# One weight tile in four of a feed-forward stage: its lower part by an accumulating DMA instead of a VectorE subtraction

## The chip, the cores and the metric

The kernel runs on one core of a Trainium2 chip. A core has five engines with queues of their own: TensorE (PE; PEld is its loading of the stationary operand), VectorE (DVE), ScalarE (ACT), GpSimd (POOL) and SyncE (SP, which here only starts DMAs). 16 DMA engines move data between the chip's memory and the core's SBUF. The metric is the time of one execution on the device in microseconds (us); less is better.

## The reference

One layer of a hybrid decoder over 256 positions with a model width of 2048, all in float32. A state-space group and an attention group work on one joint input projection and share an output projection; then comes a feed-forward part with a short causal convolution between its two matrices, then a gated embedding. The part that matters here:

```
a    = RMSNorm(h)
h    = h + concat(ssd_heads, attn_heads) @ W_out
g, u = split(causal_dwconv3(RMSNorm(h) @ W_up))       # W_up: 2048 x 11264
h    = h + (SiLU(g) * u) @ W_down                     # W_down: 5632 x 2048
h    = h + sigmoid(RMSNorm(h) @ W_pg) * RMSNorm(p @ W_pe)
```

## The kernel before

**Split products.** TensorE works on float32r, a rounded float32. To keep the precision of float32, each operand is split into a rounded upper part and the rest, the lower part, and three products are added: upper × upper, upper × lower and lower × upper. The activations are split once and stay in SBUF (`Lhs`, hi and lo). The weights are split tile by tile as they arrive.

**A weight tile.** `load_w` fetches 128 partitions x 1024 floats (512 KB): two blocks of 128 rows by 512 columns of a weight matrix. SP starts the load into `w`, for which there are `WR` = 7 buffers. `split` then has ScalarE copy it, rounding, to `wh` (line 192), and VectorE subtract: `wl = w - wh` (line 193). `wh` and `wl` have `WB` = 4 buffers each. `products` issues 12 matmuls of 512 columns for a tile: 2 blocks × 2 halves of the positions × 3 products (lines 222 to 224: upper × `wh`, upper × `wl`, lower × `wh`).

**A chunk.** `gemm` runs a list of tiles into one pair of PSUM accumulators (one for each 128 positions; two such pairs exist). In the up projection a chunk is 512 columns of W_up: eight tiles, numbered s = 0 to 7. There are 22 chunks, 11 for g and 11 for u. After a chunk, `up` scales the accumulators to `u` on ScalarE (line 879), and GpSimd separates the 16-bit halves into `half` (line 881). SP starts two DMA transposes into `flip` (line 883), GpSimd puts the halves together again in `uc` (line 884), and ScalarE and VectorE do the convolution (lines 286 and 288). For a pair of chunks GpSimd multiplies SiLU(g) by u (line 904), and the result is split for the down projection.

**Segments.** `SEGS` = 2, 2, 2, 2, 2, 1 pairs of chunks. The down projection of a segment (`project`: four columns of 512, with four tiles each for two pairs and two tiles each for one) is taken up after the chunks of the next segment; the last one follows at the end, in a call of its own.

**Order.** Each engine carries out its queue in order. In this stage the order in each queue is made by a scheduler when the program is built: it simulates the program in time and gives each engine what is ready. A buffer's next writer waits until its last reader is done. Only the attention stage and the start have TensorE's order written by hand.

Of the kernel before, what the change touches and what calls it, by code (L numbers as in the profile page):

```python
# [11 lines left out]
F32 = mybir.dt.float32  # L12
# [3 lines left out]
AF = mybir.ActivationFunctionType  # L16
ALU = mybir.AluOpType
# [7 lines left out]
KT = D // P  # L25
EPS = 1e-6
NC = 512
KG = 4
KW = 2
# [36 lines left out]
def hybrid_layer(  # L66
# [20 lines left out]
    nc = tc.nc  # L87
    V, S, G, PE = nc.vector, nc.scalar, nc.gpsimd, nc.tensor
# [19 lines left out]
    def sb(pool, shape, tag, dt=F32, bufs=None):  # L108
        kw = {} if bufs is None else {"bufs": bufs}
        size = math.prod(shape[1:]) * (2 if dt in (mybir.dt.bfloat16, U16) else 4)  # L110
        tags = sizes.setdefault(pool.id, {})
        tags[tag] = max(tags.get(tag, 0), -(-size // 32) * 32 * (bufs or pool.bufs))
        return pool.tile(shape, dt, tag=tag, name=nm(tag), **kw)
# [7 lines left out]
    def acc_pair():  # L121
        return [ps_acc.tile([P, NC], F32, tag=f"acc{b}", name=nm(f"acc{b}")) for b in range(NB)]
# [17 lines left out]
    def load_first(k, pieces=1):  # L140

        xt = sb(xin, [P, T], "xt", bufs=6)
        nc.sync.dma_start(xt, xT[:, k, :])
        w = sb(wp, [P, KW, NC], "w", bufs=WR)
        n = KW // pieces
        for c in range(0, KW, n):
            cs = slice(c, c + n)
            nc.sync.dma_start(w[:, cs, :], w_in[cs, k // KW, :, (k % KW) * NC : (k % KW + 1) * NC].rearrange("c p n -> p c n"))
        return w, xt
# [40 lines left out]
    def split(src, hi, lo, scale=None):  # L190
        if scale is None:
            S.copy(hi, src)  # L192
            V.tensor_tensor(out=lo, in0=src, in1=hi.bitcast(F32), op=ALU.subtract)  # L193
        else:
            S.activation(out=hi, in_=src, func=AF.Copy, scale=scale)
            V.scalar_tensor_tensor(out=lo, in0=src, scalar=scale, in1=hi.bitcast(F32), op0=ALU.mult, op1=ALU.subtract)

    def load_w(src, kt=KW, pieces=1):

        w = sb(wp, [P, KW, NC], "w", bufs=WR)  # L200
        wh = sb(wp, [P, KW, NC], "wh", F32R)
        wl = sb(wp, [P, KW, NC], "wl", F32R)
        n = kt * NC // pieces
        w2, wh2, wl2 = (t.rearrange("p a b -> p (a b)") for t in (w, wh, wl))
        for i in range(pieces):
            s = slice(i * n, (i + 1) * n)
            nc.sync.dma_start(w2[:, s], src[:, s])
            split(w2[:, s], wh2[:, s], wl2[:, s])
        return wh, wl

    def products(acc, lhs, w, k0, kt, total, apart=False, halves=False, whole=None):

        wh, wl = w
        order = [(i, b) for i in range(kt) for b in range(NB)]
        if apart:
            order.sort(key=lambda ib: ib[1])
        if halves:
            order = order[:kt]
        for i, b in order:
            k = k0 + i  # L220
            hi, lo = lhs(k, b)
            PE.matmul(acc[b], lhsT=hi, rhs=wh[:, i, :], start=(k == 0), stop=False)  # L222
            PE.matmul(acc[b], lhsT=hi, rhs=wl[:, i, :], start=False, stop=False)  # L223
            PE.matmul(acc[b], lhsT=lo, rhs=wh[:, i, :], start=False, stop=(k == total - 1 or (b == NB - 1 and k + 1 == whole)))  # L224
        if halves:
            b = NB - 1
            for c in range(0, NC, NC // 2):
                cs = slice(c, c + NC // 2)
                for i in range(kt):
                    hi, lo = lhs(k0 + i, b)  # L230
                    for left, right in ((hi, wh), (hi, wl), (lo, wh)):
                        PE.matmul(
                            acc[b][:, cs],
                            lhsT=left,
                            rhs=right[:, i, cs],
                            start=False,
                            stop=True,
                            skip_group_check=True,
                        )

    def gemm(acc, lhs, srcs, halves=False):

        for s, src in enumerate(srcs):
            last = s == len(srcs) - 1
            total = len(srcs) * KW
            products(acc, lhs, load_w(src), s * KW, KW, total, last, last and halves, total - KW if halves else None)

    class Lhs:

# [59 lines left out]
    def v3(a, m):  # L309
        return a.rearrange("p (a b) -> p a b", a=m)  # L310
# [7 lines left out]
    with xin_:  # L318
# [21 lines left out]
        for k in range(KT):  # L340
            w, xt = first[k] if k < len(first) else load_first(k)
# [6 lines left out]
            wh = sb(wp, [P, KW, NC], "wh", F32R)  # L348
            wl = sb(wp, [P, KW, NC], "wl", F32R)
            n = 1 if k < 3 else KW  # L350
# [12 lines left out]
            if k in (5, 9):  # L363
                b = k // 4 - 1
# [15 lines left out]
    def in_chunk(c):  # L380
        acc = acc_pair()
        gemm(acc, aT, [w_in[c, g] for g in range(KT // KW)])
        return acc

    def evac_scaled(acc, pool, tag, bufs=None):
        res = []
        for b in range(NB):
            t = sb(pool, [P, NC], f"{tag}{b}", bufs=bufs)
            S.activation(out=t, in_=acc[b], func=AF.Copy, scale=rx[:, b : b + 1])
            res.append(t)  # L390
        return res

    def add_to_h(acc, n):
        for b in range(NB):
            hs = hres[b][:, n * NC : (n + 1) * NC]
            V.tensor_tensor(out=hs, in0=hs, in1=acc[b], op=ALU.add)  # L396
# [10 lines left out]
        V.tensor_reduce(out=s1, in_=ss, axis=AX.X, op=ALU.add)  # L407
        return rstd(s1, D, NB, tag)

    def project(lhs, w, i0, ni, after=None):  # L410

        for n in range(4):
            acc = acc_pair()
            gemm(acc, lhs, [w[i, n] for i in range(i0 * KG // KW, (i0 + ni) * KG // KW)])
            add_to_h(acc, n)
            if after:
                after(n)
# [3 lines left out]
    with tc.tile_pool(name="ssd", bufs=1) as sp, tc.tile_pool(name="dram", bufs=1, space=bass.MemoryType.DRAM) as dp:  # L421
        BT = sb(sp, [P, 4, T], "BT")
        CT = sb(sp, [P, 4, T], "CT")
        for c, (acc, dst, tag) in enumerate(((acc_b, BT, "ct"), (acc_c, CT, "Xd"))):
            t = evac_scaled(acc, sp, tag, 1)
# [9 lines left out]
        for b in range(NB):  # L435
            V.scalar_tensor_tensor(
                out=u[:, :, b, :], in0=v3(tr[:, b * 32 : (b + 1) * 32], 4), scalar=rx[:, b : b + 1], in1=v3(dtb, 4), op0=ALU.mult, op1=ALU.add
# [21 lines left out]
        for b in range(NB):  # L459
            V.scalar_tensor_tensor(  # L460
                out=adt4[:, :, b, :], in0=dt4[:, :, b, :], scalar=-1.0, in1=v3(ea, 4), op0=ALU.mult, op1=ALU.mult
# [174 lines left out]
    hT = Lhs(act, KT, "a")  # L636
# [234 lines left out]
    with tc.tile_pool(name="ffn", bufs=2) as fp:  # L871

        def up(c):
            acc = acc_pair()
            gemm(acc, hT, [w_up[c, g] for g in range(KT // KW)])
            uc = sb(fp, [P, 4, T], "uc", bufs=1)
            for b in range(NB):
                u_ = sb(fp, [P, NC], f"u{b}", bufs=1)
                S.activation(out=u_, in_=acc[b], func=AF.Copy, scale=rh[:, b : b + 1])  # L879
                half = sb(fp, [P, 2 * NC], f"half{b}", U16, 1)  # L880
                G.tensor_copy(half.rearrange("p (a n) -> p a n", a=2), u_.bitcast(U16).rearrange("p (n a) -> p a n", a=2))  # L881
                flip = sb(fp, [P, 8, P], f"flip{b}", U16, 1)
                nc.sync.dma_start_transpose(flip, half)
                G.tensor_copy(  # L884
                    uc[:, :, b * P : (b + 1) * P].bitcast(U16).rearrange("p f (t a) -> p f t a", a=2),
                    flip.rearrange("p (a f) t -> p f t a", a=2),
                )
            cv = sb(fp, [P, 4, T], f"cv{c // NPAIR}", bufs=2 - c // NPAIR)
            for f in range(4):
                w = fcw[:, (4 * c + f) * 4 : (4 * c + f + 1) * 4]  # L890
                conv_tile(uc[:, f, :], cv[:, f, :], [w[:, j : j + 1] for j in range(3)], w[:, 3:4])
            return cv

        pair = 0
        pending = []
        ssg = sb(small, [P, NB, 4], "ssg", bufs=1)

        for s, np_ in enumerate(SEGS):
            gT = Lhs(fp, KG * np_, "g")
            for i in range(np_):  # L900
                cg = up(pair + i)
                S.activation(out=cg, in_=cg, func=AF.Silu)
                cu = up(NPAIR + pair + i)
                G.tensor_tensor(out=cg, in0=cg, in1=cu, op=ALU.mult)
                split(cg, gT.t[i][0], gT.t[i][1])
            if pending:
                project(*pending.pop())
            pending.append((gT, w_down, pair, np_))
            pair += np_
        h2T = Lhs(act, KT, "a")  # L910
        project(*pending.pop(), lambda n: next_lhs(h2T, ssg, n, g_ple))
        embed()
    rg = finish_rstd(ssg, "rg")


    with tc.tile_pool(name="ple", bufs=2) as lp:
# [5 lines left out]
        for n in range(4):  # L922
            acc = acc_pair()
# [77 lines left out]
```

## Time and profile before

| | |
|---|---|
| Median of 3 runs | 1433.31 us (1432.83 to 1434.88) |
| Profiled execution, its span | 1434.9 us |
| TensorE matmul busy | 1423.2 us (99%) |
| VectorE, ScalarE, GpSimd busy | 984.1, 804.2, 286.2 us |
| HBM read, written | 268.32 MB, 2.13 MB |

The span is the time from the first to the last instruction of the profiled execution, 1434.9 us, which is its own time here, against the runs' median of 1433.31 us. In the lists below, a group of instructions has a line number of the kernel, an engine, an operation, the tiles written and read, its count, its busy time with the mean length in ns of one, and the idle time of the engine just before them with what ended it. A timeline row has the start and length in us. A matmul's length there is that of the whole pipeline; TensorE issues the next one before it is over.

### The profile page before, as it was taken

What the parts mean: (1) busy time and instruction counts of PE and PEld (TensorE: products, weight loads), DVE (VectorE), ACT (ScalarE), POOL (GpSimd) and SP (SyncE); (2) the same over time, 40 slices, a digit from 0 to 9 for tenths busy, and PEclk for the clock granted to TensorE, in tenths of its full rate; (3) what the DMA queues carried; (4) which work ended last, traced back from release to release, by engine and by line L of the source; (5) the groups of instructions that cost most, each with busy time, mean ns of one, the idle gap of its engine ahead of it and who ended that gap; (6) DMA issues with size and microseconds to landing.
All of it is one profiled execution on the core that took longest, in us unless ns stands there. A gap on an engine that the chain in (4) does not pass through costs nothing.

```text
span 1434.9 us, 18092 instructions
## 1 busy us (share of the span) xinstructions
PE 1423.2 (99%) x6527; PEld 1167.3 (81%) x6527; DVE 984.1 (69%) x1242; ACT 804.2 (56%) x1101; POOL 286.2 (20%) x212
## 2 busy tenths in 40 slices
PE   9999999999999999999999999999999999999998
PEld 7887888888787778888888888888888888888887
DVE  6678876776678897656667646765675576476854
ACT  6675555644567666556556446545554554455643
POOL 0002010008345432013243112201320131120000
PEclk9999999999999999999999999999999999999999
DMA  9656656548687778577887767867876877776671
GB/s 332 236 173 198 215 177 185 171 148 223 188 220 187 209 220 220 168 211 207 219 226 202 217 205 206 225 196 198 230 208 192 223 201 218 206 208 190 208 226 65
DMA packets 163467, 292.62 MB, mean 204 GB/s; under 512 B 93041, under 2 KB 95921, under 8 KB 162993
## 3 DMA queue, kind: packets, MB, share of 16 engines
q1 hardware_dynamic: 162944, 290.99, 70.5%
q8 instruction: 51, 0.84, 0.2%
q10 hardware_dynamic: 432, 0.48, 0.1%
q14 instruction: 40, 0.32, 0.1%
HBM read 268.32 MB, written 2.13 MB: 188 GB/s over the span
## 4 chain that ended last, share of the span: by engine, by line
PE 68%; DVE 1%; ACT 0%; issue 0%; POOL 0%; DVEq 0%; ACTq 0%
PE acc L222 22%; PE acc L224 22%; PE acc L223 22%; PE tr L779 1%; PE tr L272 0%; PE sc L738 0%; DVE wl L193 0%; ACT s L753 0%; DVE nm L749 0%; DVE s L742 0%; ACT wh L192 0%; DVE sg L931 0%; ACT s L761 0%; DVE qkr L672 0%; DVE h L396 0%
## 5 line engine op out<-in xcount | busy, mean ns | idle before, releaser
L193 DVE TENSOR_TENSOR wl<-w,wh 128x1024 fp32r<-128x1024 f32 (+1 forms) x495 | 634.9, 1288 | 378.5 <-ACT wh L192 376.4
L192 ACT CAST wh<-w 128x1024 fp32r<-128x1024 f32 (+1 forms) x495 | 514.8, 1045 | 480.7 <-PE acc L224 431.4
L223 PE MATMUL acc<-wl,ah 128*128 128x512 f32 x1278 | 500.1, 391 | 1.5 <-DVE wl L193 1.5
L224 PE MATMUL acc<-wh,al 128*128 128x512 f32 x1278 | 499.0, 391 | 0.0
L222 PE MATMUL acc<-wh,ah 128*128 128x512 f32 x1278 | 498.3, 392 | 0.0
L223 PEld LDWEIGHTS acc<-wl,ah 128*128 128x128 f32 x1278 | 240.1, 188 | 52.3 <-DVE wl L193 2.4
L222 PEld LDWEIGHTS acc<-wh,ah 128*128 128x128 f32 x1278 | 240.1, 188 | 51.0 <-issue 1.4
L224 PEld LDWEIGHTS acc<-wh,al 128*128 128x128 f32 x1278 | 240.1, 188 | 50.1 <-issue 0.7
L224 PE MATMUL acc<-wh,gl 128*128 128x512 f32 x352 | 137.1, 390 | 0.0
L223 PE MATMUL acc<-wl,gh 128*128 128x512 f32 x352 | 137.1, 390 | 0.0
L222 PE MATMUL acc<-wh,gh 128*128 128x512 f32 x352 | 136.5, 390 | 0.0
L881 POOL COPY half<-u 128x1024 uint16<-128x1024 uint16 x44 | 62.0, 1422 | 264.3 <-ACT u L879 264.3
L222 PE MATMUL acc<-wh,yh 128*128 128x512 f32 x256 | 101.6, 397 | 0.6 <-DVE h L396 0.6
L223 PE MATMUL acc<-wl,yh 128*128 128x512 f32 x256 | 99.9, 390 | 0.0
L224 PE MATMUL acc<-wh,yl 128*128 128x512 f32 x256 | 99.7, 390 | 0.0
L884 POOL COPY uc<-flip 128x1024 uint16<-128x1024 uint16 x44 | 54.9, 1248 | 177.2 <-DMA flip<-half 174.9
L223 PEld LDWEIGHTS acc<-wl,gh 128*128 128x128 f32 x352 | 66.1, 188 | 13.7
L224 PEld LDWEIGHTS acc<-wh,gl 128*128 128x128 f32 x352 | 66.1, 188 | 13.6
L222 PEld LDWEIGHTS acc<-wh,gh 128*128 128x128 f32 x352 | 66.1, 188 | 13.6
L288 DVE SCALAR_TENSOR_TENSOR cv<-uc,fcw,cv 128x254 f32<-128x254 f32 (+1 forms) x176 | 73.2, 476 | 3.4 <-ACT cv L286 3.4
L396 DVE TENSOR_TENSOR h<-h,acc 128x512 f32<-128x512 f32 x112 | 73.0, 678 | 1.8 <-PE acc L224 1.8
L222 PEld LDWEIGHTS acc<-wh,yh 128*128 128x128 f32 x256 | 48.1, 188 | 14.6 <-issue 2.0
(239 smaller groups left out, 1129.2 us busy)
## 6 DMA issues: line engine op xcount, KB each, us to landing
w<-in_w_up_dram SPq DMA_DIRECT2D x176, 512.0 KB, 4.2
w<-in_w_in_dram SPq DMA_DIRECT2D x126, 512.0 KB, 4.2
w<-in_w_down_dram SPq DMA_DIRECT2D x88, 512.0 KB, 4.3
w<-in_w_out_dram SPq DMA_DIRECT2D x64, 512.0 KB, 4.2
w<-in_w_pg_dram SPq DMA_DIRECT2D x32, 512.0 KB, 4.3
seg<-scr SPq DMA_DIRECT2D x8, 512.0 KB, 5.0
xt<-in_xT_dram SPq DMA_DIRECT2D x16, 128.0 KB, 7.0
h<-in_x_dram SPq DMA_DIRECT2D x2, 1024.0 KB, 8.7
```

Of the source, the lines that this page charges most:

```text
L192: S.copy(hi, src)
L193: V.tensor_tensor(out=lo, in0=src, in1=hi.bitcast(F32), op=ALU.subtract)
L222: PE.matmul(acc[b], lhsT=hi, rhs=wh[:, i, :], start=(k == 0), stop=False)
L223: PE.matmul(acc[b], lhsT=hi, rhs=wl[:, i, :], start=False, stop=False)
L224: PE.matmul(acc[b], lhsT=lo, rhs=wh[:, i, :], start=False, stop=(k == total - 1 or (b == NB - 1 and k + 1 == whole)))
L288: V.scalar_tensor_tensor(out=dst[:, s:], in0=ps[:, : T - s], scalar=taps[n - 1 - s], in1=dst[:, s:], op0=ALU.mult, op1=ALU.add)
L396: V.tensor_tensor(out=hs, in0=hs, in1=acc[b], op=ALU.add)
L779: PE.matmul(v3(o[e * HD : (e + 1) * HD, kv * 2 * P : (kv + 1) * 2 * P], 2), lhsT=v[kb][:, vs], rhs=pT[e][:, :, kb, :], start=(kb == 0), st ...
L881: G.tensor_copy(half.rearrange("p (a n) -> p a n", a=2), u_.bitcast(U16).rearrange("p (n a) -> p a n", a=2))
L884: G.tensor_copy(uc[:, :, b * P : (b + 1) * P].bitcast(U16).rearrange("p f (t a) -> p f t a", a=2), flip.rearrange("p (a f) t -> p f t a", ...
```

## The change

`load_w` gets a marker, `by_dma`. Where it is set, ScalarE rounds `w` to `wh` and then writes a second, scaled copy, `wl = -wh`. GpSimd then starts a DMA that reads `w` and adds it on to `wl` in SBUF. VectorE has no part in such a tile. `gemm` sets the marker for the tiles with s % 4 = 3, where its caller passes `by_dma=3`: all up chunks, and the down projections inside the loop over the segments, but not the last one. All other calls, and the other tiles, are split as before. `load_w` also loses the arguments `kt` and `pieces`, whose defaults all its callers used.

```
-    def load_w(src, kt=KW, pieces=1):
+    def load_w(src, by_dma=False):
 
         w = sb(wp, [P, KW, NC], "w", bufs=WR)
         wh = sb(wp, [P, KW, NC], "wh", F32R)
         wl = sb(wp, [P, KW, NC], "wl", F32R)
-        n = kt * NC // pieces
-        w2, wh2, wl2 = (t.rearrange("p a b -> p (a b)") for t in (w, wh, wl))
-        for i in range(pieces):
-            s = slice(i * n, (i + 1) * n)
-            nc.sync.dma_start(w2[:, s], src[:, s])
-            split(w2[:, s], wh2[:, s], wl2[:, s])
+        nc.sync.dma_start(w.rearrange("p a b -> p (a b)"), src)
+        if by_dma:
+            S.copy(wh, w)
+            S.activation(out=wl, in_=wh.bitcast(F32), func=AF.Copy, scale=-1.0)
+            G.dma_start(out=wl, in_=w, accum_op=ALU.add)
+        else:
+            split(w, wh, wl)
         return wh, wl
...
-    def gemm(acc, lhs, srcs, halves=False):
+    def gemm(acc, lhs, srcs, halves=False, by_dma=None):
...
-            products(acc, lhs, load_w(src), s * KW, KW, total, last, last and halves, total - KW if halves else None)
+            products(acc, lhs, load_w(src, s % 4 == by_dma), s * KW, KW, total, last, last and halves, total - KW if halves else None)
...
-    def project(lhs, w, i0, ni, after=None):
+    def project(lhs, w, i0, ni, after=None, by_dma=None):
...
-            gemm(acc, lhs, [w[i, n] for i in range(i0 * KG // KW, (i0 + ni) * KG // KW)])
+            gemm(acc, lhs, [w[i, n] for i in range(i0 * KG // KW, (i0 + ni) * KG // KW)], by_dma=by_dma)
...
-            gemm(acc, hT, [w_up[c, g] for g in range(KT // KW)])
+            gemm(acc, hT, [w_up[c, g] for g in range(KT // KW)], by_dma=3)
...
-                project(*pending.pop())
+                project(*pending.pop(), by_dma=3)
```

## The prediction

> **What bounds the kernel now.** I read the page first: the span, the busy engines, the chain that ended last.
>
> ```profile
> span 1434.9 us, 18092 instructions
> PE 1423.2 (99%) x6527; PEld 1167.3 (81%) x6527; DVE 984.1 (69%) x1242; ACT 804.2 (56%) x1101; POOL 286.2 (20%) x212
> PE 68%; DVE 1%; ACT 0%; issue 0%; POOL 0%; DVEq 0%; ACTq 0%
> ```
>
> TensorE carries the chain; VectorE has 1% of it although it is busy for 69%. A busy matmul row is not proof of a full TensorE, so the second view is the stretches of the feed-forward stage, which runs from about 614 to 1330 us: all but its end, its first up-projection chunks, a stretch inside one down projection, and a single slice.
>
> ```profile
> core 0: us, PE busy (x) PEld busy (x) DVE busy (x) ACT busy (x) POOL busy (x), PEclk, DMA share, GB/s
> 614.00:1285.00 671.00, 671.00 (x2966) 556.06 (x2965) 429.40 (x475) 352.13 (x408) 151.52 (x100) 1.00 0.77 211
> 614.00:780.00 166.00, 166.00 (x738) 137.57 (x737) 109.16 (x121) 95.03 (x117) 50.65 (x32) 1.00 0.81 216
> 820.00:840.00 20.00, 20.00 (x90) 16.59 (x89) 10.21 (x10) 7.87 (x8) 0.00 (x0) 1.00 0.65 193
> ```
>
> 671.00 busy of 671.00 us, at a granted clock of 1.00: there is no idle time here to win. The DMA engines are at 0.81 where chunks of the up projection bring transposes beside the weights, and 0.65 with weights alone. In the whole run the matmuls that read the lower parts waited this much for VectorE:
>
> ```profile
> PE acc L223 <- DVE wl L193: 1.5, 2, 1.0
> ```
>
> So a weight tile can only cost time, by being late. The third view is the timeline of one chunk boundary, for how early a tile is made and when it is needed (start us, length us, engine).
>
> ```profile
> 1001.47 0.39 PE L222 MATMUL acc<-wh,ah 128*128 128x512 f32 x1
> 1009.63 0.39 PE L222 MATMUL acc<-wh,ah 128*128 128x512 f32 x1
> 1009.64 0.19 PEld L223 LDWEIGHTS acc<-wl,ah 128*128 128x128 f32 x1
> ...
> 1000.90 1.05 ACT L902 ACTIVATE cv<-cv 128x1024 f32<-128x1024 f32 x1
> 1001.85 0.68 ACT L879 ACTIVATE u<-acc,rh 128x512 f32<-128x512 f32 x1
> 1002.41 1.05 ACT L192 CAST wh<-w 128x1024 fp32r<-128x1024 f32 x1
> 1004.39 1.05 ACT L192 CAST wh<-w 128x1024 fp32r<-128x1024 f32 x1 [0.93 <-PE acc L224]
> 1012.55 1.05 ACT L192 CAST wh<-w 128x1024 fp32r<-128x1024 f32 x1 [1.66 <-PE acc L224]
> ...
> 1003.50 1.28 DVE L193 TENSOR_TENSOR wl<-w,wh 128x1024 fp32r<-128x1024 f32 x1 [2.23 <-ACT wh L192]
> ```
>
> The chunk's first matmul is issued at 1001.47. The one of its fourth tile (s = 3) comes at 1009.63: three tiles in 8.16 us, 2.72 us a tile of 12 matmuls (issued every 0.227 us; 0.39 is the pipelined length). There are four buffers for wh and wl, so ScalarE rounds tile k only when TensorE has left tile k-4: the copies are released by "PE acc". Tile s = 3's copy is the one at 1002.41 (0.7 us late, behind u at 1001.85), s = 4's that at 1004.39, s = 7's that at 1012.55. The lower part of s = 3 is asked for at 1009.64 and is now ready at 1003.50 + 1.28 = 1004.78, 4.9 us ahead. That margin is what the change spends.
>
> **The change part by part.** It touches 64 tiles: s = 3 and 7 in each of 22 up chunks (44), and s = 3 in the four columns of five down projections of four tiles (20). The last down projection has two tiles a column and no marker.
>
> Removed: 64 subtractions on VectorE.
>
> ```profile
> L193 DVE TENSOR_TENSOR wl<-w,wh 128x1024 fp32r<-128x1024 f32 x489 | 630.8, 1295 | 375.8 <-ACT wh L192 373.7 <-DMA w<-in_w_out_dram 1.1
> L192 ACT CAST wh<-w 128x1024 fp32r<-128x1024 f32 x489 | 511.1, 1050 | 476.9 <-PE acc L224 431.4 <-issue 21.4 <-PE acc L329 5.9
> ```
>
> 64 × 1.295 = 83 us of VectorE work goes. It gains nothing: VectorE is busy 429 of 671 us there and TensorE waits for nothing.
>
> Added on ScalarE: 64 scaled copies. I price each as the rounding copy of that size, 1.05 us: 67 us in all, which takes ScalarE from 352 to about 419 of 671 us. It idles 1.66 us before an undisturbed copy, which hides the next tile's work, but the tile's own lower part waits for it: two neighbouring 1024-wide operations start 0.95 us apart (1000.90, 1001.85), so the negated tile of s = 3 is complete at 1002.41 + 0.95 + 1.05 = 1004.41, that of s = 7 at 1014.55.
>
> Added on GpSimd's queue: 64 DMA issues, each waiting for that copy. The instructions there now, in the same chunk:
>
> ```profile
> 1001.13 1.04 POOL L881 COPY half<-u 128x1024 uint16<-128x1024 uint16 x1 [9.34 <-ACT u L879]
> 1002.65 1.04 POOL L881 COPY half<-u 128x1024 uint16<-128x1024 uint16 x1 [0.48 <-ACT u L879]
> 1008.16 1.16 POOL L884 COPY uc<-flip 128x1024 uint16<-128x1024 uint16 x1 [4.47 <-DMA flip<-half]
> 1013.43 1.17 POOL L884 COPY uc<-flip 128x1024 uint16<-128x1024 uint16 x1 [4.11 <-DMA flip<-half]
> 1022.02 3.26 POOL L904 TENSOR_TENSOR cv<-cv,cv 128x1024 f32<-128x1024 f32 x1 [7.43 <-DVE cv L288]
> 1031.26 1.23 POOL L884 COPY uc<-flip 128x1024 uint16<-128x1024 uint16 x1 [2.01 <-DMA flip<-half]
> ```
>
> GpSimd is free from 1003.69 to 1008.16 and, but for the uc copy, from 1009.3 on, so both DMAs can be issued at once if they stand there in the queue; I take that. Behind them wait the uc copies and the convolution that reads uc. That convolution would have to slip by most of the time from 1014.60 to the next chunk's uc at 1031.26 before its single buffer matters, so a slip of a microsecond or two is hidden.
>
> The new wait is TensorE's, for the accumulating DMA. No such DMA, and none issued by GpSimd, is in this trace. The nearest rows are those of loads (KB each, us from issue to landing), first of the stage, then of the whole run, then SP's time to issue:
>
> ```profile
> w<-in_w_up_dram SPq DMA_DIRECT2D x166, 512.0 KB, 4.3
> flip<-half SPq DMA_TRANSPOSE x44, 5.4
> ...
> w<-in_w_down_dram SPq DMA_DIRECT2D x88, 512.0 KB, 4.3
> ppg<-in_ppg_dram SPq DMA_DIRECT2D x1, 1024.0 KB, 5.6
> h<-in_x_dram SPq DMA_DIRECT2D x2, 1024.0 KB, 8.7
> ...
> 1001.29 0.33 SPq L207 DMA_DIRECT2D w<-in_w_up_dram  x1
> 1002.20 1.24 SPq L883 DMA_TRANSPOSE flip<-half  x1
> ```
>
> It writes 512 KB and reads 1024 KB (w, and wl to add to). Low: a plain 512 KB load, 4.3, and an issue of 0.33, together 4.6 us. High: the slowest 1 MB row, 8.7, and 1.24, together 9.9. I take the 1 MB row of 5.6, as it reads that much, and about 1.0 for an issue by GpSimd, nearer the transpose's than the plain load's: 6.6 us.
>
> What it may last: s = 3 is needed at 1009.64, so 1009.64 - 1004.41 = 5.23 us; s = 7 at 1009.64 + 4 × 2.72 = 1020.52, so 5.97 us. The fourth tile of a down projection's first column meets the same u copies, so 5.23; the other columns 5.97. That makes 27 tiles with 5.23 and 37 with 5.97. Late by 1.37 and 0.63 us: 27 × 1.37 + 37 × 0.63 = 37 + 23 = 60 us. Nothing gives this back: while TensorE stands, it frees no buffer, so the following tile of this kind starts as much later. Low end: nothing late, 0. High end: 27 × 4.67 + 37 × 3.93 = 272 us.
>
> [...]
>
> DMA time: weights alone take 0.65 of 2.72 us, 1.77 us a tile. An accumulate costs as much (one stream) to twice that (two reads), so two a chunk add 3.5 to 7.1 us to 21.76, or 0.16 to 0.33 to the 0.81. At 1.14 the DMA engines would stretch a chunk by 3.0 us, 67 us over 22 chunks: no more than the late tiles cost already, and the same time, so it isn't added.
>
> The tile w is held until the DMA has read it, 2.0 + 6.6 = 8.6 us after the copy's start rather than 2.4. There are seven such buffers: its refill, needed 7 × 2.72 = 19.0 us after that start, has 10.4 us for a landing of 4.3. Hidden; with 6 us more it would not be. SP's later loads and flips may slip behind it, covered by the same slack as uc.
>
> Sum: +60 us on the profile's 1434.9, which lies 1.6 above the median of 1433.3 (within its runs, 1432.8 to 1434.9): 1493.
>
> **The rivals.** First, the other side: the DMA lands in time. For it: a weight load of 4.3 us already shares the queues with transposes, and 4.6 is under 5.23. It decides where issue and landing together stay under 5.2 us for nearly every tile; an average lateness of 0.045 us is already 2.9 us. Against: the doubled reads, and transposes of 5.4 us in flight just where s = 3 is made. Time: 1433, no change; the freed VectorE is worth nothing. Second: the scheduler puts the DMA of s = 3 behind the first uc copy, which waits for a flip until 1008.16. Issued at 1009.32, it is 1009.32 + 6.6 - 1009.64 = 6.3 us late in 22 chunks, 4.9 more than above: 108 us, so 1601. Against: half copies were already put ahead of uc copies. Third: the accumulate is slow in itself, the high end: 1433 + 272 = 1705. Fourth: another order of instructions happens to win a few microseconds outside the stage, near 1428; nothing in the trace speaks for it.
>
> **How the numbers follow.** About 0.2% (2.9 us) is what a measurement of this kernel can tell from no change. Moderate lateness, my forecast: 0.48, with 1440 to 1560 as its own range. In time: 0.22. Behind uc: 0.13. Slow in itself: 0.13. Faster by chance: 0.04. Slower is 0.48 + 0.13 + 0.13 = 0.74. The range goes from 1432 (no change) to 1620, which leaves out the slow accumulate's upper part and the lucky order.
>
> **What would show it.** Right: waits of TensorE at L223 for a DMA on wl, some 64 of them, 0.6 to 1.4 us each; ScalarE 67 us busier, VectorE 83 us less; accumulates landing 5 to 7 us after the scaled copy. In time: the stage still without a gap. Behind uc: waits of 6 us, only at s = 3. The prediction is wrong if the DMA lands in under 5 us, or if TensorE's order was arranged so that other matmuls fill the wait.

## The result, and the profile after

The changed kernel takes 1501.45 us (median of 4 runs, 1496.34 to 1505.69) against 1434.10 us (1432.83 to 1434.89) on the same chip: 1.0468 times as long, 95% interval 1.0449 to 1.0486. Forecast were 1493 us, 1432 to 1620.

The page of the profiled execution, first the rows that answer to those of before, then its queues and the rows of the new operations (busy, mean ns of one, idle time before them and its releaser):

```profile
span 1499.4 us, 18291 instructions
PE 1446.3 (96%) x6527; PEld 1176.2 (78%) x6527; DVE 916.7 (61%) x1178; ACT 867.3 (58%) x1165; POOL 321.5 (21%) x276
PE 52%; DMA 12%; DVE 3%; ACT 2%; issue 2%; POOL 0%; SPq 0%; ACTq 0%; DVEq 0%; POOLq 0%
...
q1 hardware_dynamic: 162944, 290.99, 62.9%
q0 software_dynamic: 9216, 33.56, 11.9%
...
L193 DVE TENSOR_TENSOR wl<-w,wh 128x1024 fp32r<-128x1024 f32 (+1 forms) x431 | 559.9, 1308 | 446.3 <-ACT wh L192 444.3
L224 PE MATMUL acc<-wl,ah 128*128 128x512 f32 x1278 | 509.1, 399 | 39.7 <-DMA wl<-w 39.4
L207 POOL DMA_DIRECT2D wl<-w x64 | 55.7, 870 | 268.0 <-ACT wl L206 195.4
```

The added operations cost what was forecast: ScalarE is 867.3 - 804.2 = 63.1 us busier, VectorE 984.1 - 916.7 = 67.4 us less (the 64 subtractions are gone, 634.9 - 559.9 = 75.0 us in their group; the remaining ones got longer). TensorE does the same 6527 matmuls, but the chain that ended last now has 12% of DMA in it, where it had none. What TensorE waits for, in the waits (us in total, times, longest):

```profile
PEld acc L224 <- DMA wl<-w: 49.7, 22, 6.2
PE acc L224 <- DMA wl<-w: 40.6, 16, 5.8
```

Line 224 is the old 223, the matmul that reads the lower part. This view has waits of over 0.15 us: 16 for the accumulating DMA, not some 64, and of 2.5 us on average, not 0.6 to 1.4. The tile view of `wl` has the accumulates themselves (duration in ns, minimum/median/maximum; then issue to landing in us):

```profile
L206 ACT ACTIVATE wl<-wh x64: 1045/1061/1064, 613.2 to 1364.0; 128x1024 fp32r<-128x1024 f32 x64
L207 POOL DMA_DIRECT2D wl<-w x64: 855/866/1080, 614.6 to 1365.3; - x64
...
DMA to landing us min/median/max: 4.4/5.4/8.9
```

The stage, in stretches (as before: busy us of PE, PEld, DVE, ACT, POOL, then the granted clock, the DMA share, GB/s):

```profile
614.00:1350.00 736.00, 692.64 (x2956) 564.23 (x2955) 357.95 (x407) 411.50 (x467) 185.59 (x160) 0.97 0.84 235
640.00:680.00 40.00, 40.00 (x176) 32.74 (x176) 17.43 (x19) 24.95 (x28) 9.86 (x11) 1.00 0.92 244
880.00:920.00 40.00, 34.71 (x133) 28.01 (x133) 16.48 (x23) 19.70 (x25) 9.70 (x9) 0.87 0.67 191
```

The loss is uneven. From 640 to 680 TensorE doesn't miss a matmul (176 in 40 us, one each 0.227 us) although the DMA engines are at 0.92; from 880 to 920 it does only 133, and its granted clock is 0.87. So neither the DMA engines' total nor every marked tile is what costs.

Each of the 64 tiles can be followed if TensorE's instructions are laid beside the order in the built program, which names the buffers. A wait is then what an issue interval has beyond 0.227 us, so short waits that the view leaves out count too:

| tiles | waits | us |
|---|---|---|
| s = 3 of the up chunks | 16 of 22 | 42.0 |
| s = 7 of the up chunks | 2 of 22 | 0.6 |
| down projections | 2 of 20 | 1.6 |
| matmuls at half clock behind such waits | 8 times | about 17 |
| waits for other things in the stage | | 2.9 |

Together 64 us, against 1499.4 - 1434.9 = 64.5 us between the two spans.

Here is one bad boundary, chunk 9, in the timeline (start, length):

```profile
870.79 1.04 ACT L205 CAST wh<-w 128x1024 fp32r<-128x1024 f32 x1
871.73 1.05 ACT L192 CAST wh<-w 128x1024 fp32r<-128x1024 f32 x1
872.68 1.05 ACT L206 ACTIVATE wl<-wh 128x1024 fp32r<-128x1024 f32 x1
...
874.03 0.87 POOL L207 DMA_DIRECT2D wl<-w  x1 [1.97 <-PE acc L225]
...
874.07 3.45 SPq L203 DMA_DIRECT2D w<-in_w_up_dram  x2
...
880.83 0.80 PE L224 MATMUL acc<-wl,ah 128*128 128x512 f32 x1 [3.64 <-DMA wl<-w]
881.42 0.63 PE L225 MATMUL acc<-wh,al 128*128 128x512 f32 x1
881.85 0.63 PE L224 MATMUL acc<-wl,ah 128*128 128x512 f32 x1
882.28 0.63 PE L225 MATMUL acc<-wh,al 128*128 128x512 f32 x1
```

Three things are to be seen. ScalarE puts the next tile's rounding copy (871.73) between this tile's copy and its negation, so the negated tile is complete at 873.73, 2.94 us after the copy's start instead of 2.15. The DMA is issued at 874.03 and lands 6.75 us later. TensorE, which had come to this tile's lower part at 877.04, stands until 880.83, and then its matmuls follow each other every 0.43 us instead of 0.227.

The granted clock is 0.5 for 3.4 or 6.8 us at eight of the nine waits of more than 2 us, beginning between 2.0 us before the wait's end and 0.5 us behind it. The starts of these eight stretches lie whole multiples of 3.41 us apart, and in the 3.41 us before each of them TensorE stood for at least 2.04 us (chunk 15). The ninth wait, 3.66 us in chunk 17, lies on both sides of such a point of time, 1.90 us before and 1.76 us behind it, and the clock stays at 1.00.

The missing waits at s = 7 and in the down projections are seen at the end of chunk 8:

```profile
865.47 0.39 PE L225 MATMUL acc<-wh,al 128*128 128x512 f32 x1
865.70 1.07 PE L223 MATMUL acc<-wh,ah 128*128 128x512 f32 x4
866.61 0.39 PE L224 MATMUL acc<-wl,ah 128*128 128x512 f32 x1
```

Ahead of 865.70 lines 223, 224 and 225 alternate; there four matmuls of line 223 follow each other. The scheduler, which simulates the program when it makes the queues, does other matmuls first and comes to the lower part of s = 7 at 867.74, 2.04 us after the tile's first matmul. Over all chunks it puts s = 7 off by 4.07 us on average and the down tiles by 4.93 us, filling in with the next chunk's or column's first matmuls, which go to the other pair of accumulators. Tile s = 3 sits inside a chunk, whose matmuls it keeps in order; it is put off 0.45 us.

GpSimd's queue has a part as well. In chunks 7, 15 and 19 the DMA of s = 3 stands behind the multiplication of line 905 (2.4 us) and is issued 2.4 to 2.7 us after the negation; these three tiles wait 7.7 of the 42 us.

### The profile page after: what moved, and what is told of

Its sections match the earlier page's. It is cut to its first block, busy times and chain, and to the rows that moved or that the text cites. A ratio compares the mean times of both kernels' runs of the same rounds, so it can differ in the third digit from the quotient of the medians.

```text
span 1499.4 us, 18291 instructions
## 1 busy us (share of the span) xinstructions
PE 1446.3 (96%) x6527; PEld 1176.2 (78%) x6527; DVE 916.7 (61%) x1178; ACT 867.3 (58%) x1165; POOL 321.5 (21%) x276
## 3 DMA queue, kind: packets, MB, share of 16 engines
q0 software_dynamic: 9216, 33.56, 11.9%
## 4 chain that ended last, share of the span: by engine, by line
PE 52%; DMA 12%; DVE 3%; ACT 2%; issue 2%; POOL 0%; SPq 0%; ACTq 0%; DVEq 0%; POOLq 0%
PE acc L224 17%; PE acc L225 17%; PE acc L223 17%; DMA wl<-w 8%; DMA flip<-half 3%; DVE wl L193 1%; ACT wh L205 1%; ACT wl L206 1%; PE tr L780 1%; ACT wh L192 0%; PE sc L739 0%; PE tr L273 0%; POOL uc L885 0%; DVE cv L289 0%; DMA w<-in_w_up_dram 0%
## 5 line engine op out<-in xcount | busy, mean ns | idle before, releaser
L193 DVE TENSOR_TENSOR wl<-w,wh 128x1024 fp32r<-128x1024 f32 (+1 forms) x431 | 559.9, 1308 | 446.3 <-ACT wh L192 444.3
L192 ACT CAST wh<-w 128x1024 fp32r<-128x1024 f32 (+1 forms) x431 | 446.4, 1044 | 335.0 <-PE acc L225 296.2
L224 PE MATMUL acc<-wl,ah 128*128 128x512 f32 x1278 | 509.1, 399 | 39.7 <-DMA wl<-w 39.4
L225 PE MATMUL acc<-wh,al 128*128 128x512 f32 x1278 | 505.3, 396 | 0.0
L223 PE MATMUL acc<-wh,ah 128*128 128x512 f32 x1278 | 488.1, 395 | 0.6 <-DVE h L397 0.6
L205 ACT CAST wh<-w 128x1024 fp32r<-128x1024 f32 x64 | 67.1, 1049 | 119.3 <-PE acc L225 81.6
L223 PE MATMUL acc<-wh,gh 128*128 128x512 f32 x352 | 126.9, 391 | 2.5 <-DVE h L397 1.4
L207 POOL DMA_DIRECT2D wl<-w x64 | 55.7, 870 | 268.0 <-ACT wl L206 195.4
L289 DVE SCALAR_TENSOR_TENSOR cv<-uc,fcw,cv 128x255 f32<-128x255 f32 (+1 forms) x176 | 73.8, 486 | 46.3 <-ACT cv L287 46.2
L885 POOL COPY uc<-flip 128x1024 uint16<-128x1024 uint16 x44 | 60.6, 1386 | 176.5 <-DMA flip<-half 176.3
```

Of the source, the lines that this page charges most:

```text
L205: S.copy(wh, w)
L207: G.dma_start(out=wl, in_=w, accum_op=ALU.add)
L289: V.scalar_tensor_tensor(out=dst[:, s:], in0=ps[:, : T - s], scalar=taps[n - 1 - s], in1=dst[:, s:], op0=ALU.mult, op1=ALU.add)
L885: G.tensor_copy(uc[:, :, b * P : (b + 1) * P].bitcast(U16).rearrange("p f (t a) -> p f t a", a=2), flip.rearrange("p (a f) t -> p f t a", ...
```

## The experiments

All times are medians against the kernel before on the same chip (1434.0 to 1434.5 us), with a 95% interval of the ratio. The scheduler makes the queues anew for each kernel, so that a run can differ from the change in its order too.

**Parts of the change alone.** Theory 1 is the reading of the profile after, that only tiles inside a chunk wait; rival 3 is the prediction's step, that each tile is late by its own amount.

One place of the three at a time, first s = 7 (`by_dma=7` compared with s itself in `up`, none in `project`):

```
-            products(..., load_w(src, s % 4 == by_dma), ...)
+            products(..., load_w(src, s == by_dma), ...)
-            gemm(acc, hT, [...], by_dma=3)
+            gemm(acc, hT, [...], by_dma=7)
-                project(*pending.pop(), by_dma=3)
+                project(*pending.pop())
```

> Only the eighth tile (s = 7) of each of the 22 up chunks goes by DMA. Theory 1 (only s = 3 of an up chunk can be late, because its remaining matmuls all add into the same two accumulators, while the scheduler puts those of s = 7 behind matmuls of the next chunk): no change, 1433 to 1438 us, and no wait of TensorE for wl over 0.5 us. Rival 2 (the extra DMA traffic, GpSimd work and ScalarE work cost the time, whoever waits): 22 of 64 tiles, about a third of +66, so near 1456. Rival 3 (the step on record: each tile is late by its own 0.63 us): 22 x 0.63 = +14, so 1448.

1451.78 us (1442.44 to 1458.45), 1.0110 (1.0067 to 1.0153). Theory 1 expected no change: missed. The runs scatter around both rivals (1448 and 1456), so they don't tell these two apart. The profiled run, the fastest of the four, shows two waits:

```profile
PE acc L224 <- DMA wl<-w: 4.6, 2, 2.5
...
DMA to landing us min/median/max: 4.6/5.4/11.5
```

Both come from landings of 11.35 and 11.50 us with two transposes in flight. What the longer runs waited for stays open, as no profile shows them.

s = 3 alone (the same `s == by_dma`, with `by_dma=3` in `up` and none in `project`):

> Only the fourth tile (s = 3) of each up chunk goes by DMA. Theory 1: nearly the whole loss, +50 to +66, so 1483 to 1500 us, with 15 or so waits of TensorE and the clock at half after those over 3.4 us. Rival 2: a third of it, near 1456. Rival 3: 22 x 1.37 = +30, so 1464.

1449.50 us (1448.48 to 1450.58), 1.0097 (1.0080 to 1.0113). Missed by far: theory 1 expected 1483 at least, since the waits of the change are nearly all at s = 3, and the rivals, 1456 and 1464, lie above it too. Here only 8 of the same 22 tiles wait, 12.1 us in all, and the clock is halved once. No run shows 3.4 us as the length over which a wait halves the clock: in the change six of the seven waits over 3.4 us brought half clock, and so did two shorter ones, of 3.27 and 2.04 us. The waits here:

```profile
PE acc L224 <- DMA wl<-w: 10.7, 7, 4.6
```

The down projections alone (`up` without marker):

> Only the last tile of the columns of the five down projections goes by DMA (20 tiles). Theory 1: 0 to +5 us, 1433 to 1439. Rival 2: 20 of 64 tiles, near +20, so 1454. Rival 3: 5 x 1.37 + 15 x 0.63 = +16, so 1450.

1436.04 us (1434.45 to 1437.37), 1.0009 (1.0000 to 1.0018), and no wait for `wl`: as theory 1 expected, and under the rivals' 1454 and 1450, by which each accumulate would cost something. The three parts add up to 17.3 + 15.0 + 1.5 = 34 us, half of the change's 67. Something between the parts costs the rest.

**Two parts together.** s = 3 and s = 7, no down tiles:

```
-                project(*pending.pop(), by_dma=3)
+                project(*pending.pop())
```

> s = 3 and s = 7 of each up chunk go by DMA, the down projections don't (44 tiles). Apart they cost +15 (s = 3) and +17 us (s = 7). Theory 1b (the scheduler puts off the matmuls that need s = 7's lower part, so its buffer comes free later, and the next s = 3, which takes that buffer, has less lead): much more than the sum, +45 to +65 us, 1480 to 1500. Rival 2b (each accumulate loads the DMA engines and the effects add): +32, so 1467.

1493.84 us (1488.91 to 1499.33), 1.0412 (1.0379 to 1.0444): 59 us, where the two parts add up to 32. It is the interplay, as theory 1b had it, and not the sum. s = 3 waits 15 times for 37.9 us, s = 7 twice for 4.4:

```profile
PE acc L224 <- DMA wl<-w: 39.6, 16, 4.3
```

The rows of each tile say how. With s = 7 put off, TensorE leaves that tile's buffers later, and the next marked tile, s = 3 of the following chunk, is the one that takes one of them. From the finished negation to its first use it has 5.49 us on average when s = 3 is marked alone and 4.68 us in the change; and the time from the negation to the landing grows from 5.64 to 6.38 us. Worked out tile by tile, s = 3 is late by 11.7 us in all with both sets of numbers from s = 3 alone, 25.3 with the change's leads, 27.4 with its landings, 41.3 with both. So about half each; that division is arithmetic on rows, not an experiment. Nor is the lost lead all TensorE's: in the five worst chunks it falls from 5.7 to 3.1 to 3.3 us, and 0.8 us of that is the rounding copy that ScalarE puts ahead of the negation.

**The traffic without the wait.** The negation and the accumulate go to a tile that nobody reads; VectorE subtracts as before:

```
+            V.tensor_tensor(out=wl, in0=w, in1=wh.bitcast(F32), op=ALU.subtract)
+            spare = sb(spares[0], [P, KW, NC], "spare", F32R, 1)
-            S.activation(out=wl, in_=wh.bitcast(F32), func=AF.Copy, scale=-1.0)
-            G.dma_start(out=wl, in_=w, accum_op=ALU.add)
+            S.activation(out=spare, in_=wh.bitcast(F32), func=AF.Copy, scale=-1.0)
+            G.dma_start(out=spare, in_=w, accum_op=ALU.add)
```

> All 64 tiles get their lower part from VectorE again; the scaled copy and the accumulating DMA are still made, into a spare tile that nobody reads. The DMA traffic, the issues on GpSimd and the copies on ScalarE stay; TensorE's wait for the DMA goes. Theory 1 (the wait is the cost): 1433 to 1440 us. Rival 2 (traffic, GpSimd's queue or ScalarE's time is the cost): most of +66 stays, 1480 to 1500.

1446.31 us (1434.89 to 1456.01, ten runs), 1.0081 (1.0046 to 1.0117): above theory 1's range, far below rival 2's. The spare tile has one buffer, for which ScalarE waits once in the profiled run, 0.9 us. The profiled run is one of the short ones:

```profile
span 1433.4 us, 18381 instructions
...
spare<-w POOLq DMA_DIRECT2D x64, 512.0 KB, 5.7
```

The 64 accumulates land in 5.7 us (median), and TensorE's granted clock is 1.00. So ScalarE's work, GpSimd's issues and the DMA traffic are hidden in this run. In the median 12 of the 67 us stay, so TensorE's wait for the DMA is most of the change's cost. Eight of the ten runs lose 7 to 22 us; their granted clock is 0.994 to 0.999, against 1.000 in the two short ones, but no profile shows what TensorE waited for in them.

**Where the time of the DMA goes.** A plain DMA in place of the adding one:

```
-            G.dma_start(out=wl, in_=w, accum_op=ALU.add)
+            G.dma_start(out=wl, in_=w)
```

> The accumulate is left out: the same DMA from GpSimd copies w over wl (so the lower part is wrong), everything else, the scaled copy before it too, stays. In the changed kernel a 4 KB packet of the accumulate takes 328 ns at the median, one of a weight load 159. If the second read is what makes the tile late (theory 1), packets fall to about 160 ns, the landing from 5.4 to near 4.1 us, and the time to 1433 to 1450. If the issue through GpSimd and the queueing are (rival), the landing stays over 5 us and the time over 1475.

1481.97 us (1480.74 to 1483.76), 1.0329 (1.0314 to 1.0344). The landings got short, as theory 1 had it, the time stayed in the rival's range:

```profile
L207 POOL DMA_DIRECT2D wl<-w x64: 537/538/779, 614.6 to 1346.2; - x64
...
DMA to landing us min/median/max: 2.8/3.7/15.0
```

s = 3 still waits 20.5 us in 7 chunks, and s = 7 10.6 us twice, for landings of 15.0 and 12.8 us. The packets tell the two parts of a landing apart. A packet of 4 KB takes 328 ns (median) when it adds, 174 ns in the plain copy, 159 ns in a weight load, so the add nearly doubles it; a second read and the adding itself are not told apart here. Without the add, whose issue on GpSimd is also longer (0.87 against 0.54 us), the time is 1501.45 - 1481.97 = 19 us shorter, of the 67. The rest of a landing is before the first packet: with free queues it comes 1.44 us after the issue (plain: 1.11), but up to 4.8 us after where SP starts a weight load or transposes just before it or at the same moment, as at 874.07 above (3.34 us). A plain DMA has it too (up to 5.2 us). The fastest landings are 2.8 us here and 4.4 in the change, the medians 3.7 and 5.4.

**The order of TensorE.** The change, with TensorE's queue of the stage in the order of the program:

```
+        with tc.manual_schedule(engines={PE.engine}):
             for s, np_ in enumerate(SEGS):
```

> The change, but TensorE's instructions of the feed-forward stage keep the order of the program, so nothing is put off. From the landings of the changed kernel, held against the place in that order: s = 7 would be late in 14 of 22 tiles by 42 us in all, the down tiles in 17 of 20 by 50 us. Theory 1b: the waits of s = 3 shrink to those it has alone (12 us), but s = 7 and the down tiles wait 40 to 90 us, and the clock halves more often: 1500 to 1550. Rival 4 (the new order is itself what costs): below 1480.

1490.83 us (1489.94 to 1491.66), 1.0390 (1.0374 to 1.0405): neither theory's range. The waits spread to all three places, as the prediction had them:

```profile
PEld acc L224 <- DMA wl<-w: 52.7, 36, 7.4
PE acc L224 <- DMA wl<-w: 38.1, 25, 7.0
```

By place: 17.5 us in 14 at s = 3, 14.9 in 10 at s = 7, 10.9 in 7 in the down projections, and about 8 us of half clock. So putting off s = 7 and the down tiles removes 25.8 - 2.2 = 23.6 us of waits there and brings 24.5 us more at s = 3, with more of them long enough to halve the clock. The waits are nearly the same, 43.3 us here and 44.2 in the change, but the half clock costs 8 us instead of 17: in program order the change is 11 us faster than in the scheduler's. The control is the same edit on the kernel before:

> The kernel before with TensorE's queue in the order of the program through the feed-forward stage, no accumulating DMA. Theory A (without the late tiles the order matters little): 1433 to 1440 us, so that the 1490.8 us of the change in this order holds 51 to 58 us of the change's. Theory B (the planner's order is worth something of itself, because the fillers of a chunk's end cover work that every chunk has): 1445 us or more, and the change's own part in program order is smaller by that much.

1434.58 us (1433.54 to 1436.06), 1.0003 (0.9993 to 1.0012). The order in itself is worth nothing; all 56 us in program order are the change's.

**More buffers.** `WB = 5` for `wh` and `wl`, and to make room `WR = 5` for `w`:

> The change with five buffers for wh and wl rather than four, and five for w rather than seven: a tile is made 2.72 us earlier before its use. Theory 1 (lead against latency): the mean lateness goes, within 8 us of before, 1433 to 1442. Rival 2 (DMA traffic or queues): still slower by half or more, over 1465.

1468.17 us (1464.62 to 1471.00), 1.0238 (1.0216 to 1.0261): theory 1 missed, in rival 2's range. The waits of s = 3 fell to 2.2 us, but s = 7 has 14.4 us in 11 tiles and the landings got longer (median 7.0 us). In all 11 the DMA stands behind `uc` in GpSimd's queue and is issued 3.9 to 6.8 us after the negation, so that here the queue is what is left. Its control, the same counts in the kernel before:

> The kernel before with the buffer counts of the fifth-buffer run and nothing else: WB=5 for wh and wl, WR=5 for w. That run took 1468.2 us, where 1442 at most was expected. Theory A (the 34 us are still the change's: with one more buffer the tiles s=3 no longer wait, but the tiles s=7 still do): this kernel stays at 1433 to 1438 us. Theory B (the raw tile's shorter ring, five buffers instead of seven, brings loads late by itself): this kernel takes 1445 to 1468 us, and the change's own part of the 34 us is what is left above it.

1440.07 us, 1.0042 (1.0025 to 1.0059), between the two theories: the shorter ring of raw tiles costs 6 us, the change with one more buffer 28, if the two add up. A buffer more takes away over half of the cost, not all.

**Another engine for the negation.** VectorE instead of ScalarE:

```
-            S.activation(out=wl, in_=wh.bitcast(F32), func=AF.Copy, scale=-1.0)
+            V.tensor_scalar_mul(wl, wh.bitcast(F32), -1.0)
```

> The change, with the negation of the rounded tile on VectorE (a multiplication by -1) instead of ScalarE. Theory A (the tile s=3 is late by what its chain takes from the freed buffer on; in the worst chunks ScalarE runs the next tile's rounding copy of about 1.05 us between the rounding copy and the negation): the negation starts right behind the copy there, about 0.9 us of lead come back in the 5 worst chunks and little elsewhere, 1480 to 1496 us. Rival B (VectorE, with its subtractions of 1.3 us and the two conversions of a chunk's end, 61% busy, makes the negation wait as long as it gains): 1496 to 1515 us. Rival C (most of the lateness is ScalarE's queue): under 1475 us.

1499.31 us (1496.53 to 1503.10), 1.0458 (1.0439 to 1.0477): in rival B's range, but not for its reason. The negation takes 0.69 us (median) instead of 1.06, and the waits at s = 3 halve to 20.8 us, but s = 7 gets 15.5 us in 12 tiles and the down projections 12.1 us:

```profile
L206 DVE TENSOR_SCALAR wl<-wh x64: 680/693/2712, 610.9 to 1365.5; 128x1024 fp32r<-128x1024 f32 x64
...
PE acc L224 <- DMA wl<-w: 43.2, 33, 3.8
```

Half as many us in each wait, twice as many waits. At s = 3 the negation does not wait as long as it gains: from the copy's start to the negated tile it is 2.15 us on average instead of 2.55, and the lead is 5.54 instead of 4.68 us. But s = 7 loses lead (8.02 instead of 9.36 us), and its DMA is issued 2.50 instead of 1.51 us after the negation. So ScalarE's queue is a part of what s = 3 waits for, and taking the negation out of it moves the waits instead of ending them.

**Other tiles.** s = 2 and 6 instead of 3 and 7 (`by_dma=2` in both calls):

> The change with the tiles s=2 and s=6 of each group of eight instead of s=3 and s=7 (up), and s=2 (down): the same 64 tiles, the same work. Theory A (a tile's lateness is set by where it stands: a tile inside a chunk can't be put off, a chunk's last tile can, and its being put off takes lead from the next accumulated tile): now no touched up tile is put off, so none frees its buffers late for the next; both s=2 and s=6 are late by little, s=2 more, where the transposes of the chunk before are in flight: about 0.5 us for each of the 44 up tiles with few waits over 2 us, so that the clock is rarely halved, and 0 to 1.4 us for each of the 20 down tiles: 1450 to 1480 us. Rival B (the place doesn't matter, only the number of accumulates): 1496 to 1506 us. Rival C (without the putting off, s=6 and the down tiles wait as s=3 does): over 1515 us.

1487.67 us (1482.43 to 1493.07), 1.0375 (1.0338 to 1.0412): above theory A's range, below B's; the profiled run is its longest, 1493.07. The sum hides two opposite places. s = 2 waits 1.4 us in 2 of 22 tiles: its DMA is issued 0.30 us behind the negation and lands in 4.62 us (median), inside a lead of 6.0 us. s = 6 waits 38.5 us in 15. In chunk 2:

```profile
661.76 1.06 ACT L206 ACTIVATE wl<-wh 128x1024 fp32r<-128x1024 f32 x1
...
665.98 1.16 POOL L885 COPY uc<-flip 128x1024 uint16<-128x1024 uint16 x1 [8.88 <-DMA flip<-half]
667.08 0.85 POOL L207 DMA_DIRECT2D wl<-w  x1
...
672.89 0.50 PE L224 MATMUL acc<-wl,ah 128*128 128x512 f32 x1 [3.23 <-DMA wl<-w]
```

The negation is done at 662.82, but the DMA stands in GpSimd's queue behind `uc`, which waits for a transpose: it is issued 4.26 us late. This is the prediction's rival "behind uc", at another place than it was put. 14 of the 15 waits at s = 6, 25.6 us, have `uc` just ahead of the DMA in GpSimd's queue and an issue 1.5 to 6.5 us late; the 15th, 12.9 us, is a landing of 21.51 us with two transposes in flight. So the accumulates were nearly free at s = 2 (1.4 us in all), and theory A's rule, by the place in the chunk alone, was wrong: what counted at s = 6 is what stood ahead of them in GpSimd's queue and in the DMA queues.

## Why the prediction was right, and where it was not

**Held.** The sign, the size (+60 forecast, +67 measured) and the mechanism: in the kernel before, TensorE had no idle time from 614 to 1285 us (busy for 671.00 of 671.00), so VectorE's saved time bought nothing and each late lower part was TensorE's loss. The spare-tile run shows that without the wait 12 of the 67 us are lost, the plain copy that the add matters, the fifth buffer that the lead matters. The added DMA share was hidden, as forecast: at 0.92 TensorE still ran without a gap.

**The price of the DMA.** Taken: 1.0 for the issue and 5.6 to land, 6.6 us, within 4.6 and 9.9. The read of 1024 KB, by which the 1 MB row was taken, is in no trace: the page counts 33.56 MB for the 64 accumulates, 512 KB each, as for the plain copies. Measured from the issue's start: 5.4 median, 4.4 to 8.9, and GpSimd's issue of 0.87 us lies inside it; 0.30 us pass from the negation to the issue where the queue is free, up to 6.5 where it isn't. From the negation to the landing the 64 tiles took 6.9 us in the middle, 4.7 to 12.4: 0.3 more than taken, but no constant. With a free queue it would be 0.3 + 5.4 = 5.7; the difference is time in GpSimd's queue. The negated tile itself came later than taken: 2.15 us after the copy's start at most tiles instead of 2.0, and 2.9 to 4.9 where ScalarE put something between. (The row at 1001.85, whose start gave the 0.95, is `u`, 512 wide and not 1024.)

**The terms of the sum.** The prediction wrote 27 tiles × 1.37 = 37 us and 37 tiles × 0.63 = 23 us. The first kind, s = 3 and the first down columns, gave 42 us at s = 3, in 16 waits of 0.2 to 6.0 us, and 0.6 us in the columns: the lead from the finished negation, taken as 5.23 us, is 3.1 to 3.3 us in five bad chunks (9, 10, 13, 17, 21) and 1.8 in chunk 0. The 37 tiles of the second kind and the down tiles together gave 2.2 us instead of 23 and more, and half clock, a term that wasn't in the sum, 17. So the step that failed is "some 64 of them, 0.6 to 1.4 us each"; the total came out near by luck, because about 21 us too much and 17 + 5 + 3 us too little nearly cancel. Where the sum's own order holds, in the run with TensorE in program order, the lead is 5.4 us and the way from the negation to the landing 5.7 us on average, and 31 of the 64 tiles wait, 43 us in all: one price for every tile misses that the waits come from the spread around it.

**"Nothing gives this back."** Half wrong. The text named the condition itself among its signs of being wrong ("if TensorE's order was arranged so that other matmuls fill the wait"), and that is what happened at s = 7 and in the down projections, 42 of the 64 tiles. The program order shows what it was worth: less than nothing, for the change is 11 us faster in it. Putting off a tile freed its buffers later for the next marked one: s = 3 had a lead of 4.68 us in the change, 5.49 when marked alone.

**The rivals.** In time: not so, though the fastest landings, 4.4 us, are inside the budget, and the down tiles alone do land in time. Behind `uc`: in the change the issue comes on average 0.6 us behind the negation at s = 3 (0.3 is the least) and 1.5 us at s = 7, where the matmuls were put off anyway; at s = 6, and at s = 7 with a fifth buffer, it decided. Slow in itself: no, 8.9 us was the longest landing of the change, though 21.5 us occurred.

**Open.** What the scattered runs of the spare-tile kernel and of s = 7 alone waited for; and the split between lost lead and longer landings, which is only worked out.

## What to carry to other kernels

Before moving work from an engine with slack on to a longer chain, compare the lead of the consumer with the whole chain (engine, queue position, DMA start, data), tile by tile and at its worst places, not with a mean landing. Here a tile finished late held its buffers and shortened the lead of the next one (4.68 us instead of 5.49 at s = 3), and parts that cost 34 us apart cost 67 together: time the parts alone and together. A wait of a few microseconds on TensorE cost more than its length: at eight of the nine waits of over 2 us in the change its clock was at 0.5 for 3.4 or 6.8 us, about 17 us in all.

## What the runs showed of the hardware that was not expected

- In the change TensorE's granted clock fell to 0.5 for 3.4 or 6.8 us at eight of the nine waits of more than 2 us; matmuls then were 0.43 us apart instead of 0.227. That is 17 us, a quarter of the loss. It fell at points whole multiples of 3.41 us apart, where TensorE had stood for at least 2.04 of the 3.41 us before; a wait of 3.66 us that such a point cuts into 1.90 and 1.76 us left the clock at 1.00.
- In the change an accumulating DMA issued by GpSimd had its first packet 1.44 us after the issue with free queues (1.42 to 1.48 at 30 of the 64), but up to 4.8 us after it beside a weight load or transposes just started on the other queue.
- With two transposes in flight single accumulates of 512 KB took 11.35 and 11.50 us (s = 7 alone) and 21.51 us (s = 2 and 6), where 5.4 and 4.9 us are the medians.
